# Operations put at the end of a step, and a 512-column matmul for both weight parts, in a hybrid decoder layer

## The chip, the cores and the metric

The kernel runs on one core of a Trainium2 chip. The metric is the device time of one execution in microseconds (us); the time of a version is the median of its runs. Engines are called TensorE (PE; its weight loads are PEld), VectorE (DVE), ScalarE (ACT), GpSimd (POOL) and the sync engine (SP), whose queue issues all transfers of this kernel.

## What is computed

One layer of a decoder over one prompt of 2048 tokens and eight sampled sequences of four tokens. Cut to what matters:

```python
mod = jnp.dot(jax.nn.silu(c), w_ada) + b_ada            # conditioning: shift, scale, gate
shift, scale, gate = jnp.split(mod, 3, axis=-1)
h = _rms(x, norm_g) * (1 + scale[:, None]) + shift[:, None]
proj = jnp.dot(h, w_in) + b_in                          # (T, 1024) x (1024, 7176)
hq, hf, hi, hz, mu, mz, mo, mi, mf = jnp.split(proj, SPLIT_IDX, axis=-1)
f = lb + (1.0 - lb) * jax.nn.sigmoid(hf)
o_h, S_new = _hgrn2(hq, jnp.log(f), hi, S_h, chunk)     # 8 heads, state 128 x 128
y_h = _head_rms(o_h, hgrn_norm_g) * jax.nn.silu(hz)
xc = jax.nn.silu(conv(mu) + conv_b)
q, k, v = _blockdiag(xc, wq), _blockdiag(xc, wk), _blockdiag(mu, wv)
h_m, C_new, n_new, m_new = _mlstm(q, k, v, mi, log_sigmoid(mf), C_m, n_m, m_m, chunk)  # 4 heads, 256 x 256
y_m = (_head_rms(sigmoid(mo) * h_m, mnorm_g) + skip * xc) * jax.nn.silu(mz)
out = x + gate[:, None] * jnp.dot(jnp.concatenate([y_h, y_m], -1), w_out)
```

## The kernel before

Every operand of the large products is held as two parts, a high part rounded to the matmul format and a low part that is the rest. A product is then three matmuls: high by high, low by high, high by low.

The prompt goes in four segments of 512 tokens, each in chunks of 128. A segment is a list of units. A narrow unit projects 128 columns of w_in (f, q, z, mu, mz) with the weights as the stationary operand and 512 tokens moving (`proj_ct`, line 543). A wide unit (v, mo) projects 256 columns with 128 tokens of h as the stationary operand and 256 columns of weights moving (`proj_tok`, line 556); its result is read by one addition of the bias (`evac`, line 1484), and the bias is loaded at the start of the unit into a tile with one buffer (`bias_bc`, line 1370). In one of the four head groups of a segment the 32 sampled tokens ride along. Weights are split in the first segment by ScalarE and GpSimd (`split`, line 205), kept in DRAM and read back in the later ones; four slots (tag w8) hold them, of which a wide unit takes two: one for the high part and one for the low part.

The order of the work is set by hand. `run_unit` steps the matmuls of a unit; after each step `pump` (line 576) first issues stores that are due and then lets every generator in `rec` go on to its next `yield`. The heads of both branches are such generators (`hgrn`, `hgrn_out`, `conv`, `mlstm`, `mlstm_out`), so the operations of several heads stand between the matmuls of a step, on every engine in the order in which the generators issue them, and each engine takes its instructions in order. All PSUM tiles come from one ring of eight banks (`ps_tile`).

```python
for g in list(rec):
    if next(g, "end") == "end":
        rec.remove(g)
```

Before the first unit the conditioning is computed (`ada_rows`, line 451): 16 pieces of w_ada, each split by ScalarE and by VectorE or GpSimd, two accumulators of 512 columns for each half, then the rows are transposed to columns (`ada_shift_scale`), x is scaled by GpSimd (`x_scale`), transposed, and modulated (`x_modulate`), and the weights of unit 0 are split (`stream_unit(0)`, line 1588). In the HGRN2 heads the state goes from chunk to chunk by an addition on VectorE and a scaling on GpSimd (`pscale`, lines 676 to 678). The block-diagonal weights are spread out by `bd_fill` on VectorE in the first segment (`bd_prep`). At the end of a segment x of the next one is loaded and scaled (`x_next`, line 1666) while the last unit runs. After the last segment the output projection follows (line 1743).

Of the kernel before, what the change touches and what calls it, by code (L numbers as in the profile page):

```python
# [8 lines left out]
F32 = mybir.dt.float32  # L9
# [8 lines left out]
P = 128  # L18
# [49 lines left out]
def hymba_step(ctx, tc, flag, halved, x_prompt, x_sample, c_prompt, c_sample, state_hgrn, state_C, state_n, state_m,  # L68
# [140 lines left out]
    class Unit:  # L209
# [11 lines left out]
        def alloc(self):  # L221
            if self.wide:
                self.hi = ring.tile([P, KD, 2 * P], F32R, tag="w8", name="whi", bufs=4)
                self.lo = ring.tile([P, KD, 2 * P], F32R, tag="w8", name="wlo", bufs=4)
                self.parts = [x.rearrange("p k m -> p (k m)") for x in (self.hi, self.lo)]
# [10 lines left out]
        def split(self, j):  # L236
# [4 lines left out]
            split(self.raw.pop(j), self.hi[:, :, c], self.lo[:, :, c], pool if self.src is w_in else vec)  # L241
# [7 lines left out]

    def C(nm, k):  # L250
        return cols[:, col[nm] + k:col[nm] + k + 1]
# [4 lines left out]
    sct = S2("sct", [P, KD, 1 + NSEQ])  # L256
# [4 lines left out]
    vec.tensor_tensor(sct[:, :, 1:], sgc[:, KD:].rearrange("p (s k) -> p k s", k=KD),  # L261
                      acol[:, 32:96].rearrange("p (s k) -> p k s", k=KD), op=ALU.mult)

    ML = 32 + 1 + NSEQ + 1
    scs = con.tile([P, KD, ML], F32R, name="scs")
    scp = S2("scp", [P, KD, ML])
    vec.memset(scp, 0.0)
    vec.tensor_copy(scs, scp)
    vec.tensor_copy(scs[:, :, :1 + NSEQ], sct)
    vec.tensor_tensor(scs[:, :, 32:33 + NSEQ], sct, scs[:, :, :1 + NSEQ].bitcast(F32), op=ALU.subtract)  # L270
# [172 lines left out]
    NB = 1 + NSEQ  # L443

    def ada_piece(n):
        k, b = divmod(n, 2)
        t = Bt("wada", [P, D]) if n % 2 else raw_tile()
        sync.dma_start(t, w_ada[k * P:k * P + P, b * D:b * D + D])
        return t

    def ada_rows(step):

        acc = [ps_tile("pada") if b % 2 else ps_tile("pada") for b in range(4)]
        raw = {n: ada_piece(n) for n in range(4)}
        for n in range(2 * KD):
            k, b = divmod(n, 2)
            step(n)
            r = raw.pop(n)
            t = ring.tile([P, 2, D], F32R, tag="w8", name="wadas", bufs=4)
            act(t[:, 0], r, AF.Copy)  # L460
            (pool if n % 4 == 3 else vec).tensor_tensor(t[:, 1], r, t[:, 0].bitcast(F32), op=ALU.subtract)
            for g in range(2):
                c = slice(512 * g, 512 * g + 512)
                for y in range(2):
                    pe.matmul(acc[2 * b + g][:ML], scs[:, k], t[:, y, c], start=(k == 0 and y == 0),
                              stop=(k == KD - 1 and y == 1))
            if n + 4 < 2 * KD:
                raw[n + 4] = ada_piece(n + 4)
        return acc

    def ada_shift_scale(acc):
        rows = Bt("arows", [NB, D])
        rows2 = Bt("arows", [NB, D])
        for b in range(4):
            dst = (rows, rows2)[b // 2][:, 512 * (b % 2):512 * (b % 2) + 512]
            act(dst, acc[b][:NB], AF.Copy)
            vec.tensor_tensor(dst, dst, acc[b][32:32 + NB], op=ALU.add)
        for r, dst, one in ((rows, msh, 0.0), (rows2, msc, 1.0)):
            ps = ps_tile("padt")
            for k in range(KD):  # L480
                pe.transpose(ps[:, k * NB:k * NB + NB], r[:, k * P:k * P + P], ident[:NB, :NB])
            v = ps[:, :KD * NB].rearrange("p (k b) -> p k b", k=KD)
            c0 = KD if one else 0
            vec.scalar_tensor_tensor(dst, v, one, acol[:, c0:c0 + KD, None].to_broadcast([P, KD, NB]),
                                     op0=ALU.add, op1=ALU.add)
        vec.tensor_tensor(msc, msc, C8("norm_g")[:, :, None].to_broadcast([P, KD, NB]), op=ALU.mult)

    def ada_gate(g, u):
# [6 lines left out]
        for k in range(KD):  # L495
            for w in (u.hi, u.lo):
                pe.matmul(ps[:ML, :Q], scs[:, k], w[:, k, :], start=(k == 0 and w is u.hi), stop=(k == KD - 1 and w is u.lo))
# [58 lines left out]
    def proj_tok(smp, u, evac):  # L556
        for c, t0, n in toks(smp):
            ps = ps_tile("ptok")
            i = 0
            for k in range(KD):  # L560
                if n == CH:
                    for w, h in ((u.hi, hhi), (u.lo, hhi), (u.hi, hlo)):
                        pe.matmul(ps[:, :2 * P], h[:, k, t0:t0 + n], w[:, k, :], start=(i == 0), stop=(i == 3 * KD - 1))  # L563
                        i += 1
                else:
                    for w in (u.hi, u.lo):
                        pe.matmul(ps[:2 * n, :2 * P], hhi[:, k, SEG:], w[:, k, :], start=(i == 0), stop=(i == 2 * KD - 1))
                        i += 1
# [5 lines left out]
    stores = deque()  # L574

    def pump(n=1):
        for _ in range(n):
# [6 lines left out]
            for g in list(rec):  # L584
                if next(g, "end") == "end":
                    rec.remove(g)

# [13 lines left out]
    def hgrn(s, h, d):  # L601
# [10 lines left out]
        vec.tensor_tensor_scan(G[:, :W], hmask[:, :W], G[:, :W], 0.0, op0=ALU.mult, op1=ALU.add)  # L612
        g4 = G[:, :SEG].rearrange("p (c u t) -> p c u t", u=2, t=CH // 2)
        mid = small("mid", [P, NCH, 1])
        vec.tensor_copy(mid, g4[:, :, 0, CH // 2 - 1:CH // 2])
        vec.tensor_tensor(g4[:, :, 0], g4[:, :, 0], mid.to_broadcast([P, NCH, CH // 2]), op=ALU.subtract)
        pool.tensor_scalar(tn[:, :W], tn[:, :W], noml[:, h:h + 1], oml[:, h:h + 1], op0=ALU.mult, op1=ALU.add)  # L617
# [11 lines left out]
        vec.tensor_tensor(beta[:, :NCH - 1], sm[:, 0:NCH - 1], sm[:, NCH + 1:2 * NCH], op=ALU.mult)  # L629
        vec.tensor_tensor(Ep[:, :W], hq[:, :W], Ep[:, :W], op=ALU.mult)  # L630
        vec.tensor_tensor(tn[:, :W], tn[:, :W], G[:, :W], op=ALU.mult)
# [37 lines left out]
        for c in range(NCH):  # L669
# [180 lines left out]
    def hgrn_out(s, h, po, ops):  # L850
# [4 lines left out]
        for c in range(NCH):  # L855
# [3 lines left out]
        vec.tensor_tensor(on[:, :SEG].rearrange("p (c v) -> p c v", c=NCH), po.rearrange("p (c v) -> p c v", c=NCH),  # L859
                          f[:, :, None].to_broadcast([P, NCH, CH]), op=ALU.mult)  # L860
# [12 lines left out]
        vec.tensor_tensor(sz[:, :W], sz[:, :W], y[:, :W], op=ALU.mult)  # L873
# [3 lines left out]
        vec.scalar_tensor_tensor(y[:, :SEG], pn, C("hg", h), sz[:, :SEG], op0=ALU.mult, op1=ALU.mult)  # L877
        if smp:
            pn = ps_tile("pn")
            pe.matmul(pn[:, :NSM], onesm, sq)  # L880
            act(sq, pn[:, :NSM], AF.Ln, bias=epsc)
            act(sq, sq, AF.Exp, scale=-0.5)
            vec.scalar_tensor_tensor(ops, ops, C("hg", h), sq, op0=ALU.mult, op1=ALU.mult)
            vec.tensor_tensor(y[:, SEG:], ops, sz[:, SEG:], op=ALU.mult)
        y_store(s, h, y, W)
# [122 lines left out]
    def conv(s, i, j, d):  # L1008
# [28 lines left out]
        vec.tensor_tensor(xc[:, :W], xc[:, :W], e[:, :W], op=ALU.mult)  # L1037
# [55 lines left out]
    def mlstm(s, i, d):  # L1093
# [10 lines left out]
        def head(c):  # L1104
# [6 lines left out]
            vec.tensor_tensor(dm[:, t], ps[:, :CH], dm[:, t], op=ALU.mult)  # L1111
            st = small("st", [P, 2, CH], 2, F32R)
# [759 lines left out]
```

## Time and profile before

| | |
|---|---|
| median of 3 runs | 2248.98 us (2247.84 to 2250.97) |
| the profiled execution's own time | 2243.03 us |
| its span, first to last instruction | 2241.2 us |
| mean granted TensorE clock | 0.989 of full speed |

The profile is of one execution. The span leaves out what lies before the first and after the last instruction. The matmuls overlap, and their ends are modelled: the time from the start of one to the start of the next is what one costs, not its duration.

### The profile page before, as it was taken

The page shows a single profiled execution, that of the slowest core. Times are in us where ns is not written, and L with a number is a line of the kernel's source. Part 1 is how long each engine was busy: PE and PEld are TensorE (multiplying, and loading weights), DVE is VectorE, ACT ScalarE, POOL GpSimd, SP SyncE. Part 2 cuts the span into 40 slices and gives each one's busy share as a digit, 9 for nine tenths or more (in the row PEclk, how much of TensorE's full clock was granted, in tenths as well). Part 3 has the DMA queues.
Part 4 walks back from the last instruction along what each step waited for, and adds up shares of the span by engine and source line. Part 5 has one row for each costly group of instructions (what it writes and reads, how often), then busy time and mean ns, then how long its engine had stood idle before and what let it go on. Part 6 is the DMA issues. An engine that isn't in the chain of part 4 may idle for free.

```text
span 2241.2 us, 35168 instructions
## 1 busy us (share of the span) xinstructions
PE 2170.0 (97%) x13594; PEld 1915.1 (85%) x13594; DVE 1268.8 (57%) x2664; ACT 979.1 (44%) x2260; POOL 432.0 (19%) x436
## 2 busy tenths in 40 slices
PE   6999999999999999999999999999999998999998
PEld 3888998787899889899988898888899987888885
DVE  7675657566756574566574555655455675423232
ACT  6445554464443354353444454534444535212121
POOL 3424353341112020212010212110101033000000
PEclk8999999999999999999999999999999999999999
DMA  7676766864546465634465555454555566533330
GB/s 257 214 234 219 262 221 205 302 227 155 189 152 228 167 230 193 217 136 158 179 203 202 189 192 180 162 169 163 146 194 161 174 193 173 165 108 96 93 99 27
DMA packets 225318, 405.26 MB, mean 181 GB/s; under 512 B 24843, under 2 KB 168627, under 8 KB 196470
## 3 DMA queue, kind: packets, MB, share of 16 engines
q1 hardware_dynamic: 225142, 402.92, 54.2%
q8 instruction: 109, 1.79, 0.3%
q14 instruction: 67, 0.55, 0.1%
HBM read 298.43 MB, written 104.44 MB: 180 GB/s over the span
## 4 chain that ended last, share of the span: by engine, by line
PE 68%; DVE 4%; ACT 3%; DMA 1%; issue 1%; POOL 1%; SPq 0%; DVEq 0%; ACTq 0%; POOLq 0%
PE pct L549 27%; PE pout L1743 15%; PE ptok L563 11%; PE p L1151 1%; PE pc L1135 1%; PE pv L1064 1%; PE pp L663 1%; PE pa L639 1%; PE pq L1081 1%; PE po L687 1%; PE po L689 1%; PE psx L1108 1%; ACT st L92 1%; PE p L1135 1%; DMA raw<-in_w_out_dram 1%
## 5 line engine op out<-in xcount | busy, mean ns | idle before, releaser
L549 PE MATMUL pct<-hhi,w 128*128 128x512 f32 (+1 forms) x3200 | 852.0, 354 | 1.2 <-DVE S L697 1.2
L549 PEld LDWEIGHTS pct<-hhi,w 128*128 128x128 f32 x3200 | 552.9, 188 | 74.4 <-issue 3.3
L549 PE MATMUL pct<-hlo,w 128*128 128x512 f32 (+1 forms) x1600 | 560.6, 350 | 0.0
L549 PEld LDWEIGHTS pct<-hlo,w 128*128 128x128 f32 x1600 | 301.0, 188 | 39.2
L563 PE MATMUL ptok<-whi,hhi 128*128 128x256 f32 x1024 | 301.4, 294 | 4.4 <-ACT hhi L92 3.3
L563 PE MATMUL ptok<-whi,hlo 128*128 128x256 f32 x1024 | 291.2, 284 | 0.2 <-DVE hlo L426 0.2
L563 PE MATMUL ptok<-wlo,hhi 128*128 128x256 f32 x1024 | 290.9, 284 | 0.0
L1743 PE MATMUL pout<-wh,y 128*128 128x512 f32 (+1 forms) x792 | 247.2, 391 | 3.0 <-ACT wh L92 3.0
L563 PEld LDWEIGHTS ptok<-whi,hhi 128*128 128x128 f32 x1024 | 197.4, 193 | 7.8 <-ACT hhi L92 3.7
L563 PEld LDWEIGHTS ptok<-wlo,hhi 128*128 128x128 f32 x1024 | 197.6, 193 | 2.3 <-issue 2.2
L563 PEld LDWEIGHTS ptok<-whi,hlo 128*128 128x128 f32 x1024 | 197.3, 193 | 0.9 <-DVE hlo L426 0.9
L1743 PEld LDWEIGHTS pout<-wh,y 128*128 128x128 f32 (+1 forms) x792 | 148.2, 187 | 35.8 <-ACT wh L92 3.5
L1743 PE MATMUL pout<-wl,y 128*128 128x512 f32 (+1 forms) x408 | 159.8, 392 | 1.1 <-POOL wl L1780 0.6
L92 ACT ACTIVATE xo<-oo 128x512 f32<-128x512 f32 (+1 forms) x34 | 21.5, 632 | 249.5 <-DVE oo L1831 249.5
L92 ACT ACTIVATE e<-e 128x512 f32<-128x512 f32 (+1 forms) x160 | 102.0, 638 | 58.9 <-DVE e L1034 54.8
L1826 DVE TENSOR_TENSOR oo<-pout,gate 128x512 f32<-128x512 f32 x32 | 22.0, 687 | 186.3 <-PE pout L1743 185.4
L617 POOL TENSOR_SCALAR tn<-tn,noml,oml 128x512 f32<-128x512 f32 (+1 forms) x32 | 52.6, 1643 | 385.5 <-ACT G L92 384.8
L207 POOL TENSOR_TENSOR w<-raw,w 128x1024 fp32r<-128x1024 f32 x40 | 97.2, 2436 | 113.5 <-ACT w L92 95.1
L121 POOL TENSOR_SCALAR num<-num,fin 128x256 f32<-128x256 f32 x64 | 35.1, 566 | 401.7 <-DVE fin L1313 357.8
L1161 DVE SCALAR_TENSOR_TENSOR Cc<-Cc,dec,pc 128x258 f32<-128x258 f32 x120 | 52.4, 478 | 84.0 <-PE pc L1135 84.0
L1743 PEld LDWEIGHTS pout<-wl,y 128*128 128x128 f32 (+1 forms) x408 | 75.6, 185 | 19.7 <-POOL wl L1780 1.3
L1032 DVE SCALAR_TENSOR_TENSOR xc<-mu,cols,xc 128x512 f32<-128x512 f32 (+1 forms) x120 | 83.7, 698 | 4.2
(403 smaller groups left out, 3792.2 us busy)
## 6 DMA issues: line engine op xcount, KB each, us to landing
w<-wdr SPq DMA_DIRECT2D x120, 1024.0 KB
wdr<-w SPq DMA_DIRECT2D x40, 1024.0 KB
raw<-in_w_in_dram SPq DMA_DIRECT2D x56, 512.0 KB
whi<-wdr SPq DMA_DIRECT2D x24, 1024.0 KB
wlo<-wdr SPq DMA_DIRECT2D x24, 1024.0 KB
raw<-ydr SPq DMA_DIRECT2D x29, 512.0 KB
xt<-in_x_prompt_dram SPq DMA_DIRECT2D x28, 512.0 KB
raw<-in_w_ada_dram SPq DMA_DIRECT2D x16, 512.0 KB
```

The costliest lines, as they stand in the source:

```text
L92: nc.scalar.activation(out, in_, func, bias=bias, scale=scale, **kw)
L121: pool.tensor_scalar(out, in_, sc, 0.0, op0=ALU.mult, op1=ALU.add)
L207: eng.tensor_tensor(lo, raw, hi.bitcast(F32), op=ALU.subtract)
L549: pe.matmul(ps[:, :n], w[:, k, :], h[:, k, t0:t0 + n], start=(i == 0), stop=(i == 3 * KD - 1))
L563: pe.matmul(ps[:, :2 * P], h[:, k, t0:t0 + n], w[:, k, :], start=(i == 0), stop=(i == 3 * KD - 1))
L617: pool.tensor_scalar(tn[:, :W], tn[:, :W], noml[:, h:h + 1], oml[:, h:h + 1], op0=ALU.mult, op1=ALU.add)
L639: pe.matmul(pa[:, t], kt[:, t], qt[:, t])
L663: pe.matmul(pp[:, c * CH:c * CH + CH], ktT[:, c], v[:, c, vc])
L1032: vec.scalar_tensor_tensor(o, src(r), C("cw", 8 * r + k), o, op0=ALU.mult, op1=ALU.add)
L1135: pe.matmul(out[:, :DH + 2], a[:, x], b[y][:, c], start=(q == 0), stop=(q == 2))
L1161: vec.scalar_tensor_tensor(Cc[:, j], Cc[:, j], dec[:, i, c:c + 1], pcs[j][:, :DH + 2], op0=ALU.mult, op1=ALU.add)
L1743: pe.matmul(acc[g][:n if n == CH else 2 * n], a, b[:, 512 * g:512 * g + 512], start=(k == 0 and q == 0), stop=(k == KO - 1 and q == len(mm ...
```

## The change

It has these parts.

1. A wide unit's two slots hold four of the eight k each, with high and low weights side by side. A token chunk takes per k one matmul of 512 columns (both parts, with the high part of h) and one of 256 (high weights, with the low part of h). The evacuation adds the second 256 columns with an operation of its own.
2. A queue `late`: closures appended in a step run after all generators of that step. In it go the scan and what follows it, the products after the exponentials, the normalised o, the z gate and its store, the product of xc, and in the mLSTM output the scaling and the gate.
3. The chain of R scales on VectorE; the fills of `bd_prep` go to GpSimd; the mLSTM `head` issues its ScalarE and VectorE operations in another order, and takes the split of C into itself.
4. The bias of a wide unit is loaded at the end of the wide unit before.
5. `ada_rows` multiplies eight unsplit fp32 pieces of 2048 columns, four matmuls each into four groups of 32 rows of one bank; the weights of unit 0 are split on VectorE.
6. x of the next segment is scaled one call later than it is loaded, behind the modulation.

```diff
-                self.hi = ring.tile([P, KD, 2 * P], F32R, tag="w8", name="whi", bufs=4)
-                self.lo = ring.tile([P, KD, 2 * P], F32R, tag="w8", name="wlo", bufs=4)
+                self.half = [ring.tile([P, KD // 2, 2, 2 * P], F32R, tag="w8", name="wh8", bufs=4) for _ in range(2)]
...
+        def both(self, k):
+            return self.half[k // 4][:, k % 4]
...
+            if self.wide:
+                for a, t in enumerate(self.half):
+                    split(raw[:, 4 * a:4 * a + 4], t[:, :, 0, c], t[:, :, 1, c], e)
...
-        acc = [ps_tile("pada") if b % 2 else ps_tile("pada") for b in range(4)]
-        raw = {n: ada_piece(n) for n in range(4)}
-        for n in range(2 * KD):
...
+        acc = ps_tile("pada")
+        w = {k: ada_load(k) for k in range(4)}
+        for k in range(KD):
+            step(k)
+            t = w.pop(k)
+            for q in range(4):
+                pe.matmul(acc[32 * q:32 * q + 32], sct[:, k], t[:, 512 * q:512 * q + 512], start=(k == 0),
+                          stop=(k == KD - 1), skip_group_check=True)
+            if k + 4 < KD:
+                w[k + 4] = ada_load(k + 4)
...
-                    for w, h in ((u.hi, hhi), (u.lo, hhi), (u.hi, hlo)):
-                        pe.matmul(ps[:, :2 * P], h[:, k, t0:t0 + n], w[:, k, :], start=(i == 0), stop=(i == 3 * KD - 1))
+                    mm = [(hhi, w.rearrange("p a m -> p (a m)")), (hlo, w[:, 0])]
+                    for i, (h, x) in enumerate(mm if k < KD - 1 else mm[::-1]):
+                        pe.matmul(ps[:, :x.shape[-1]], h[:, k, t0:t0 + n], x, start=(k == 0 and i == 0),
+                                  stop=(k == KD - 1 and i == 1), skip_group_check=True)
...
             for g in list(rec):
                 if next(g, "end") == "end":
                     rec.remove(g)
+            while late:
+                late.popleft()()
...
+        def decays():
+            vec.tensor_tensor_scan(G[:, :W], hmask[:, :W], G[:, :W], 0.0, op0=ALU.mult, op1=ALU.add)
+            vec.tensor_copy(mid, g4[:, :, 0, CH // 2 - 1:CH // 2])
+            vec.tensor_tensor(g4[:, :, 0], g4[:, :, 0], mid.to_broadcast([P, NCH, CH // 2]), op=ALU.subtract)
+            pool.tensor_scalar(tn[:, :W], tn[:, :W], noml[:, h:h + 1], oml[:, h:h + 1], op0=ALU.mult, op1=ALU.add)
+
+        late.append(decays)
...
+        def scaled():
+            vec.tensor_tensor(beta[:, :NCH - 1], sm[:, 0:NCH - 1], sm[:, NCH + 1:2 * NCH], op=ALU.mult)
+            vec.tensor_tensor(Ep[:, :W], hq[:, :W], Ep[:, :W], op=ALU.mult)
+            vec.tensor_tensor(tn[:, :W], tn[:, :W], G[:, :W], op=ALU.mult)
+
+        late.append(scaled)
...
-                pscale(nxt, u, sc)
+                vec.tensor_scalar(nxt, u, sc, None, op0=ALU.mult)
...
+        late.append(lambda: vec.tensor_tensor(
+            on[:, :SEG].rearrange("p (c v) -> p c v", c=NCH), po.rearrange("p (c v) -> p c v", c=NCH),
+            f[:, :, None].to_broadcast([P, NCH, CH]), op=ALU.mult))
...
+        def finish():
+            vec.tensor_tensor(sz[:, :W], sz[:, :W], y[:, :W], op=ALU.mult)
+            vec.scalar_tensor_tensor(y[:, :SEG], pn, C("hg", h), sz[:, :SEG], op0=ALU.mult, op1=ALU.mult)
...
+            y_store(s, h, y, W)
...
+        late.append(lambda: vec.tensor_tensor(xc[:, :W], xc[:, :W], e[:, :W], op=ALU.mult))
...
+            def scale(nm=nm, n=n, nch=nch, f=f):
+                vec.tensor_tensor(f[:n, 3, :nch], f[:n, 2, :nch], f[:n, 1, :nch], op=ALU.mult)
+                for c in range(nch):
+                    pscale(nm[:n, c, :DH], nm[:n, c, :DH], f[:n, 3, c:c + 1])
...
+    def bias_load(u):
+        while u < len(units) and units[u][1] not in ("v", "mo"):
+            u += 1
+        if u < len(units):
+            c0 = (OI if units[u][1] == "v" else OMO) + 2 * units[u][2] * P
+            bias[u] = small("bb", [P, 2 * P], 1)
+            sync.dma_start(bias[u], bcast_ap(b_in[0, c0:c0 + 2 * P], P))
...
                     vec.tensor_tensor(t[:, c], ps[:, :2 * P], bb, op=ALU.add)
+                    vec.tensor_tensor(t[:, c], t[:, c], ps[:, 2 * P:], op=ALU.add)
...
-                bd_fill(bo[:, (k - 2) % 4, 0], 2, k - 2, vec)
+                bd_fill(bo[:, (k - 2) % 4, 0], 2, k - 2, pool)
...
-    stream_unit(0)
+    stream_unit(0, vec)
...
             nxt[c] = x_load(s + 1, c)
+
+        def x_now(c):
             x_scale(s + 1, c, nxt[c][0], nxt[c][2])
```

## Rows read from the trace of the kernel before

**Rows 1.** The page: busy time of each engine, share of the span, instructions.

```profile
PE 2170.0 (97%) x13594; PEld 1915.1 (85%) x13594; DVE 1268.8 (57%) x2664; ACT 979.1 (44%) x2260; POOL 432.0 (19%) x436
```

**Rows 2.** Windows: stretch, its us, busy us of each engine, PEclk, DMA share, GB/s.

```profile
100.00:126.00 26.00, 20.80 (x101) 17.09 (x100) 23.89 (x50) 9.52 (x19) 10.39 (x7) 0.90 0.49 122
...
300.00:400.00 100.00, 94.05 (x756) 90.56 (x755) 66.01 (x132) 52.37 (x124) 43.70 (x27) 0.98 0.76 256
...
500.00:520.00 20.00, 15.99 (x116) 15.00 (x115) 11.52 (x25) 9.39 (x24) 5.21 (x6) 0.91 0.40 164
...
600.00:1500.00 900.00, 896.46 (x6065) 813.19 (x6064) 537.89 (x1196) 418.63 (x1022) 137.68 (x189) 1.00 0.54 187
...
1500.00:1560.00 60.00, 55.77 (x352) 50.13 (x351) 33.43 (x77) 26.80 (x57) 3.60 (x6) 0.94 0.44 148
```

**Rows 3.** Waits of TensorE over the whole span: us in total, times, longest us.

```profile
PE ph L1324 <- POOL num L121: 6.7, 4, 4.2
...
PE po L689 <- DVE R L674: 4.2, 3, 3.2
PE pb L1542 <- DVE bt L1554: 4.2, 1, 4.2
...
PE pxt L397 <- POOL xt L121: 1.8, 1, 1.8
...
PE ptok L563 <- DVE y L877: 1.1, 1, 1.1
```

**Rows 4.** Timeline of the start: start us, us, engine, line, operation, idle before.

```profile
35.51 1.21 DVE L461 TENSOR_TENSOR wadas<-raw,wadas 128x1024 fp32r<-128x1024 f32 x1
35.64 4.23 PE L465 MATMUL pada<-wadas,scs 128*42 128x512 f32 x11 [3.35 <-DVE wadas L461]
...
41.54 4.65 POOL L207 TENSOR_TENSOR wlo<-raw,whi 128x1024 fp32r<-128x1024 f32 x2 [7.03 <-ACT whi L92]
...
44.01 1.37 DVE L411 TENSOR_SCALAR hst<-pxt,msc,msh 128x128 f32<-128x128 f32 x4
...
45.45 1.16 ACT L92 ACTIVATE hhi<-hst 128x512 fp32r<-128x512 f32 x2
...
46.15 0.58 PE L563 MATMUL ptok<-whi,hhi 128*128 128x256 f32 x1 [3.27 <-ACT hhi L92]
```

**Rows 5.** Timeline of TensorE from 240 us, narrow unit and token chunk.

```profile
244.59 0.62 PE L549 MATMUL pct<-hhi,w 128*128 128x512 f32 x2
...
246.66 1.88 PE L1081 MATMUL pq<-xc,bm 128*128 128x512 f32 x4
...
251.15 0.28 PE L563 MATMUL ptok<-whi,hhi 128*128 128x256 f32 x1
...
254.02 0.60 PE L1108 MATMUL psx<-qp,xc 128*128 128x128 f32 x4
```

**Rows 6.** Windows, the instructions on pout alone.

```profile
1950.00:2000.00 50.00, 50.00 (x222) 41.41 (x221) 4.12 (x6) 0.00 (x0) 1.00 0.29 84
```

**Rows 7.** Groups by line and shape: busy us, mean ns, idle before, releasers.

```profile
L677 DVE TENSOR_TENSOR U<-R,pp 128x128 f32<-128x128 f32 x120 | 34.4, 287 | 60.7 <-POOL R L121 48.7 <-PE pp L663 11.5
...
L121 POOL TENSOR_SCALAR R<-U,beta 128x128 f32<-128x128 f32 x88 | 32.7, 372 | 245.4 <-DVE U L677 243.9 <-PE pz L990 0.5 <-PE pct L549 0.5
...
L612 DVE TENSOR_TENSOR_SCAN G<-hmask,G 128x512 f32<-128x512 bf16 x24 | 29.7, 1237 | 34.9 <-ACT G L92 34.8
...
L1486 DVE TENSOR_TENSOR v<-ptok,bb 128x256 f32<-128x256 f32 x64 | 26.8, 421 | 70.3 <-PE ptok L563 36.4 <-DMA bb<-in_b_in_dram 28.9 <-PE p L1151 3.5
```

**Rows 8.** Waits of the sync queue, first 60 us.

```profile
SPq L448 <- DVE wadas L461: 9.3, 4, 4.3
```

**Rows 9.** DMA view of the first 60 us: GB/s in 40 slices.

```profile
GB/s 0 21 104 396 421 418 413 411 407 401 399 407 396 367 417 385 279 68 339 378 289 90 332 412 221 147 203 11 0 2 210 163 13 21 116 386 431 393 291 310
```

**Rows 10.** Line 331, both engines: min/median/max ns, first and last start.

```profile
L331 DVE TENSOR_TENSOR bt<-bdw,oh x16: 277/282/1957, 73.1 to 154.6; 128x128 f32<-128x128 f32 x16
...
L331 POOL TENSOR_TENSOR bdf<-bdw,oh x8: 388/487/844, 1481.9 to 1840.2; 128x128 f32<-128x128 f32 x8
```

More of the change, by code (lines that the diff above doesn't have):

```diff
@@ L441, in toks, with ada_load @@
         return [(c, c * CH, CH) for c in range(NCH)] + ([(NCH, SEG, NSM)] if smp else [])
[L443 to L448, printed above, removed]
+    def ada_load(k):
+        t = ring.tile([P, 2 * D], F32, tag="w8", name="wada", bufs=4)
+        sync.dma_start(t, w_ada[k * P:k * P + P, :2 * D])
         return t
     def ada_rows(step):
-        acc = [ps_tile("pada") if b % 2 else ps_tile("pada") for b in range(4)]
-        raw = {n: ada_piece(n) for n in range(4)}
-        for n in range(2 * KD):
[L456 to L468, printed above, removed]
@@ L473, in ada_shift_scale @@
[L473 to L485, printed above, removed]
+        r = Bt("arows", [P, 512])
@@ L495, in ada_gate @@
         for k in range(KD):
-            for w in (u.hi, u.lo):
-                pe.matmul(ps[:ML, :Q], scs[:, k], w[:, k, :], start=(k == 0 and w is u.hi), stop=(k == KD - 1 and w is u.lo))
+            for y in range(2):
+                pe.matmul(ps[:ML, :Q], scs[:, k], u.both(k)[:, y], start=(k == 0 and y == 0), stop=(k == KD - 1 and y == 1))
         yield
@@ L574, in hymba_step @@
     stores = deque()
+    late = deque()
     def pump(n=1):
@@ L1137, in mlstm @@
         cur = head(0)
-        ch = None if first else c_split()
         yield
@@ L1368, in hymba_step @@
     start.append(len(units))
-    def bias_bc(c0):
-        t = small("bb", [P, 2 * P], 1)
-        sync.dma_start(t, bcast_ap(b_in[0, c0:c0 + 2 * P], P))
-        return t
+    bias = {}
+    def bias_load(u):
[5 more added lines that the diff above has]
+            sync.dma_start(bias[u], bcast_ap(b_in[0, c0:c0 + 2 * P], P))
     KO = 2 * D // P
@@ L1415, in stream @@
                 unit.alloc()
-            unit.split(j)
+            unit.split(j, eng)
             npiece[0] += 1
@@ L1481, in run_unit @@
             ts = small(kind + "s", [P, 2 * P], 1) if smp else None
-            bb = bias_bc((OI if kind == "v" else OMO) + 2 * n * P)
+            bb = bias.pop(u)
             def evac(ps, c, w):
@@ L1497, in run_unit @@
             pump(steps)
+        if kind in ("v", "mo"):
+            bias_load(u + 1)
         if kind == "q":
@@ L1569, in x_norm, with ada_step @@
         x_scale(0, c, x0[c][0], x0[c][2])
-    def ada_step(n):
-        if n < len(row_loads):
-            sync.dma_start(*row_loads[n])
-        if n in (1, 3):
-            x0.append(x_load(0, len(x0)))
-        if n in (6, 8):
-            x_norm(n // 2 - 3)
-        if n == 13:
+    pre = []
+    def ada_step(k):
+        if k < 4:
+            for d in row_loads[4 * k:4 * k + 4]:
+                sync.dma_start(*d)
+        if k == 0:
+            x0.append(x_load(0, 1))
+        if k in (2, 4):
+            x_norm(k // 2 - 1)
+        if k == 3:
+            gate_prep()
+        if k == 4:
+            pre.extend(x_transpose(x0[0][0], CH, g) for g in range(2))
+        if k == 5:
             cols_prep()
+    x0.append(x_load(0, 0))
     acc = ada_rows(ada_step)
-    assert len(row_loads) <= 13
+    assert len(row_loads) <= 16
     load_pieces(1)
@@ L1680, in hymba_step @@
                 x_next(1)
+            if j == per - 1 and not last:
+                x_now(0)
+                x_now(1)
             if j == (5 if s == 0 else 1 if last else 2):
```

133 lines of the change are left out of this document (67 added, 66 removed).

## Prediction

> **What bounds the kernel now.** I read the page's busy line first: TensorE is busy 97% of the span, VectorE 57%, ScalarE 44%, GpSimd 19% [rows 1]. So time can come only from TensorE: fewer or cheaper matmuls, less time in which it stands still, less time at its lower clock. VectorE, ScalarE and GpSimd matter only where TensorE waits for one of them.
>
> Then the stretch table, to see where TensorE stands still. From 600 to 1500 us it is busy 896.5 of 900 us at a granted clock of 1.00: reordering other engines cannot win more than 3.5 us there [rows 2]. It loses 5.2 us in 100 to 126, 6.0 in 300 to 400, 4.0 in 500 to 520 and 4.2 in 1500 to 1560, with means of the granted clock of 0.90, 0.98, 0.91 and 0.94 [rows 2]. A mean of 0.90 is a fifth of the stretch at 1.2 instead of 2.4 GHz, 5.2 us in which half the work is done, so some 2.6 us lost; the four together give 2.6 + 1.0 + 0.9 + 1.8 = 6.3 us.
>
> Then the list of what TensorE waits for: after the start the largest are the transposes ph behind a GpSimd scaling, 6.7 us, the bd transposes' products pb behind VectorE, 4.2, po behind a VectorE R, 4.2, and pxt behind GpSimd's scaling of x, 1.8 [rows 3]. No wait for a weight load or for a bias stands among them. The last view is the timeline of the start: the first token matmul begins at 46.15 us [rows 4].
>
> **The wide matmul.** For each of 128 token chunks (16 v and 16 mo units of 4) and each of 8 k, three 256-column matmuls become one of 512 columns and one of 256. Columns stay at 768; one weight load and one matmul go, 1024 of each. A chunk of 24 runs from 251.15 to 254.02 us, so 119.6 ns from start to start [rows 5]. For 512 columns of the same kind there are two rows: nine in 2.07 us (244.59 to 246.66), 230 ns [rows 5], and 222 in 50 us of the output stage, 225 ns [rows 6]. Three at 119.6 are 358.8 ns; the new pair is 225 to 230 + 119.6 = 344.8 to 349.6. That saves 9.2 to 14.0 ns, times 1024: 9.4 to 14.3 us. I take 12.
>
> By the rows a 256-column matmul costs 119.6 ns and one of twice the width under twice that, so some 10 to 14 ns belong to each matmul whatever its width. The Trainium skill, "TensorE: Matmul & The Clock Gate", section "Back-to-back issue gap", gives a warm matmul its columns at 2.4 GHz and some 2.5 ns more; by that the saving would be 2.6 us, an estimate from the page, and the forecast some 9 us higher. The page gives that gap for matmuls by themselves, and here every matmul has a weight load of its own; the rows are of these very operations, and they decide.
>
> The evacuation now takes two VectorE additions per chunk instead of one: 128 more of 0.42 us [rows 7], 54 us of VectorE. Its cover is VectorE's idle 43%; without it a PSUM bank would come free 0.42 us later per chunk, and eight banks rotate. I charge nothing. The other bound is 0.42 x 128 = 54 us, if every bank were needed at once; the list names one wait of a token matmul for VectorE's reading of a bank, 1.1 us [rows 3], so I stay at nothing. In the first segment the splits of v and mo weights come as two of half the width on ScalarE and GpSimd, which costs their idle time; the kept copies are as many transfers of the same size as before.
>
> **The start.** Now 16 pieces of w_ada are each split by ScalarE and by VectorE or GpSimd, and the sync queue waits 9.3 us for VectorE to free buffers [rows 8]. The last eleven matmuls run from 35.64 to 39.87, the first token matmul starts at 46.15 [rows 4]. The change loads eight pieces of 1 MB into four slots and multiplies them unsplit: no ScalarE or VectorE work between landing and matmul. Transfers run at about 400 GB/s once they flow, from the fourth bin of 1.5 us [rows 9]. Ahead of the last piece's end stand 8 x 1.05 MB and two x tiles of 0.52, 9.4 MB, some 23.5 us from about 4 us on: 28 us. The last four matmuls are fp32 of 512 columns; the nearest row is pq, four of which take 1.88 us [rows 5], twice that at half clock: to 31 us with the landing. Then one copy of 512 columns (about 0.7, from 0.42 for 256 [rows 7]), four transposes (0.6, as four matmuls of 128 take [rows 5]), three small additions (under 0.3 each by the U row [rows 7]) and their hand-overs: 33.5. VectorE then also makes the low parts of the first v unit, ahead of hst: four of half the size of one that takes 1.21 us, some 2.4, where GpSimd did it beside VectorE in 4.65 us; hst 1.37 and hhi 1.16 follow [rows 4]: with a hand-over 38.5 us. Saved: 46.15 - 38.5 = 7.5, rounded. Bounds: nothing, if the first weights land or are split too late, and 11, if the split lies beside the matmuls.
>
> **Operations put at the end of a step.** Per head the scan, mid copy, subtraction and the affine of tn (GpSimd), the three products, the on product, and the gate products with their store; per conv the xc product; in the mLSTM output the kap product with four GpSimd scalings, and the gate products with their store. They are issued after all generators of the step, so VectorE no longer stands at them while ScalarE works. It stands 34.9 us before the scan now [rows 7]. That is VectorE's time, not TensorE's. Each consumer stands two or more yields behind, so TensorE pays nothing where a step has slack. Their stores, one DMA per head and per half of an mLSTM head and a second where the samples ride along, go onto the sync queue up to a step later; only the output stage reads them.
>
> **R, fills, biases, x.** 120 scalings of the R chain (88 R and 32 Sc) go from GpSimd, 372 ns for an R [rows 7], to VectorE. An addition on tiles of this size takes 287 ns there [rows 7], so about 35 us more on VectorE, against 48.7 us that it stood waiting for GpSimd's R [rows 7]. po waits shrink: of 4.2 us [rows 3] with the dip of clock behind it I count 4. Of bd_prep, 24 fills go to GpSimd, 487 instead of 282 ns by the nearest rows [rows 10], off the VectorE that is busy 23.9 of 26 us when pb waits [rows 2, 3]: of 4.2 us and 2.6 of clock I count 2, as the gate work that fills VectorE there stays. Scaling x after the modulation, not ahead of it, takes GpSimd out of a wait for the load: of 1.8 us [rows 3] and its dip I count 2. The ph wait moves 1 us either way: kap comes late, but the products ahead of it do too. The 32 bias loads move to the end of the v or mo unit before. They wait there for the last evacuation, for bb has one buffer; behind them on the sync queue stand weight loads for units to come and stores, which no TensorE wait names. Where VectorE stood for bb, 28.9 us before v alone [rows 7], it no longer does. The head's new order in the mLSTM gives ScalarE work while VectorE makes dm; TensorE waits little there, 1 us. The sum is 4 + 2 + 2 + 1 = 9, less 2 for new waits: 7. Bounds: 20, some two thirds of the 5.2 + 6.0 + 4.0 + 4.2 us of standing and 6.3 of clock in the stretches above, and a loss, the last rival below.
>
> **Sum.** 12 + 7.5 + 7 = 26.5 us. The profiled execution took 2243.0 us (span 2241.2), so 2216.5 for such an execution. The runs shown have a median of 2249.0, 6 us above it; the same saving gives 2222.
>
> **Rivals.** *The wide matmul saves nothing:* cost goes by columns, 119.6 ns for 256 and so 239 for 512. The rows at 225 and 230 speak against it, though those have another operand moving. That leaves 14.5 us: 2234. The skill's 2.5 ns per matmul would give nearly this time.
>
> *The stalls fall with the start:* the waits before 600 us and at 1543 us vanish with their clock dips, 20 us instead of 7, and the start gives 10: 12 + 10 + 20 = 42, so 2207. For it speaks that VectorE's waits for ScalarE, GpSimd and biases all shrink; against it that the ph wait of 6.7 us hangs on a chain of ScalarE and GpSimd that is as long as before.
>
> *Late reads hold PSUM (slower):* po, pn and ph are read by operations that now come last in their step, behind all of VectorE's other work: 32 + 32 + 32 banks. If the next step's matmuls need such a bank, TensorE waits. From 26.5 / 96 = 0.28 us each the change is worth nothing; at 0.5 us each it costs 48, so 2249 - 26.5 + 48 = 2270. Against it: eight banks, some two allocated per step, and VectorE idle 43%. For it: VectorE gains 54 + 35 us of work. At 0.25 us each it gives no change: 2246.
>
> **How the numbers follow.** Forecast 0.52 (own range 2212 to 2232), stalls fall 0.16, wide matmul saves nothing 0.14, late reads eat the gain 0.06, late reads cost more 0.12. Within 0.2% (4.5 us, about what a measurement can tell) is only the fourth. So faster 0.82, same 0.06, slower 0.12. The range leaves out the last two and the far end of the second: 2202 to 2241.
>
> **What would show it.** Per chunk of the token matmuls 16 matmuls in 2.76 us instead of 24 in 2.87. The first of them near 38 us. No wait of TensorE for w_ada's low parts. From 600 to 1500 us busy time still above 99%. A wait of ptok, pct or psx for y, xs or on would mean the late reads; 512-column token matmuls 239 ns apart, the first rival; a first token matmul after 44 us, that the start was bound elsewhere.

## The result and the profile after

The changed kernel takes 2215.9 us (median of 4 runs, 2212.6 to 2217.9), the kernel before 2249.4 (4 runs, 2247.8 to 2251.0): a ratio of 0.985, 95% interval 0.9833 to 0.9867. The forecast was 2222 in a range of 2202 to 2241, so the sign came out as forecast, and the time 6 us below the forecast, inside the range. Between the profiled executions the saving is 2243.0 - 2217.9 = 25.1 us, against a forecast of 26.5; between the medians it is 33.5. The two differ because the profiled execution of before lies some 5 us below its runs, while that of after is the longest of its own.

The page's busy line after, where [rows 1] had before:

```profile
PE 2152.2 (97%) x12558; PEld 1850.7 (84%) x12558; DVE 1315.6 (59%) x2884; ACT 959.9 (43%) x2264; POOL 386.0 (17%) x349
```

TensorE has 1036 instructions fewer and is still busy 97% of the span: the bound has not moved. VectorE rose by 47 us, GpSimd fell by 46.

The windows of [rows 2] again, and one more (stretch, its us, then busy us of TensorE, its weight loads, VectorE, ScalarE and GpSimd, granted clock, DMA share, GB/s):

```profile
100.00:126.00 26.00, 21.42 (x110) 18.27 (x109) 23.50 (x51) 9.72 (x26) 12.83 (x14) 0.93 0.69 186
300.00:400.00 100.00, 95.29 (x695) 88.29 (x694) 74.11 (x162) 56.56 (x142) 38.57 (x23) 0.97 0.71 235
...
500.00:520.00 20.00, 18.07 (x111) 15.70 (x110) 14.38 (x38) 10.97 (x25) 1.24 (x4) 1.00 0.32 115
100.00:600.00 500.00, 482.68 (x2899) 418.12 (x2898) 342.27 (x731) 262.49 (x608) 177.05 (x134) 0.99 0.68 228
600.00:1500.00 900.00, 895.68 (x5579) 788.65 (x5578) 584.18 (x1346) 418.65 (x1031) 113.77 (x124) 1.00 0.54 185
1500.00:1560.00 60.00, 56.24 (x281) 46.67 (x281) 30.58 (x69) 22.51 (x48) 4.45 (x7) 0.94 0.50 175
```

Most stretches still have their holes, shrunk a little: 4.6 us of standing instead of 5.2 in the first, 4.7 instead of 6.0 in the second, 3.8 instead of 4.2 in the last. Only 500 to 520 is really mended, 1.9 instead of 4.0 with the clock at 1.00. The rows compare stretches of time and not of work: after, the work lies 8 us or more earlier. From 600 to 1500 TensorE stands 4.3 us instead of 3.5: more, not less, beside a VectorE that is busy 46 us longer there.

TensorE's waits over the whole span (us in total, times, longest us), to set beside [rows 3]:

```profile
PE pb L1574 <- DVE bt L1586: 4.5, 1, 4.5
PE ph L1343 <- POOL num L121: 4.4, 3, 3.8
PE ptok L563 <- ACT hhi L92: 3.9, 2, 3.4
PE po L700 <- DVE R L685: 3.9, 2, 2.6
...
PE pa L650 <- DVE tn L640: 3.1, 3, 1.9
...
PE pxt L409 <- POOL xt L121: 0.3, 1, 0.3
```

pb and po stand where they stood (4.2 each before); pxt fell from 1.8 to 0.3, ph from 6.7 to 4.4. The wait of a token matmul for VectorE's y is gone.

The timeline of the start after, beside [rows 4]:

```profile
29.16 1.93 PE L468 MATMUL pada<-wada,sct 128*32 128x512 f32 x8 [0.68 <-DMA wada<-in_w_ada_dram]
...
33.52 0.23 DVE L485 TENSOR_TENSOR msc<-msc,cols 128x72 f32<-128x72 f32 x1
33.70 2.50 DVE L207 TENSOR_TENSOR wh<-raw,wh 128x512 fp32r<-128x512 f32 x4
...
36.12 1.36 DVE L423 TENSOR_SCALAR hst<-pxt,msc,msh 128x128 f32<-128x128 f32 x4
...
37.51 1.15 ACT L92 ACTIVATE hhi<-hst 128x512 fp32r<-128x512 f32 x2 [2.15 <-DVE hst L423]
...
38.19 0.80 PE L563 MATMUL ptok<-wh,hhi 128*128 128x512 f32 x1 [3.40 <-ACT hhi L92]
```

The times that the forecast named can be read off: the w_ada matmuls end at 31.09 (forecast 31), shift and scale at 33.75 (33.5), the low parts take 2.50 (2.4), the first token matmul starts at 38.19 (38.5).

And a token chunk on TensorE after, as [rows 5] had one:

```profile
242.44 0.39 PE L563 MATMUL ptok<-wh,hhi 128*128 128x512 f32 x1
242.67 0.28 PE L563 MATMUL ptok<-wh,hlo 128*128 128x256 f32 x1
242.78 0.40 PE L563 MATMUL ptok<-wh,hhi 128*128 128x512 f32 x1
...
245.26 0.61 PE L1125 MATMUL psx<-qp,xc 128*128 128x128 f32 x4
```

Sixteen matmuls in 245.26 - 242.44 = 2.82 us, against 24 in 2.87 before and a forecast of 2.76.

### The profile page after: what moved, and what is told of

Read it like the earlier page. It is cut to its first block, busy times and chain, and to the rows that moved or that the text cites. A ratio compares the mean times of both kernels' runs of the same rounds, so it can differ in the third digit from the quotient of the medians.

```text
span 2216.1 us, 33304 instructions
## 1 busy us (share of the span) xinstructions
PE 2152.2 (97%) x12558; PEld 1850.7 (84%) x12558; DVE 1315.6 (59%) x2884; ACT 959.9 (43%) x2264; POOL 386.0 (17%) x349
## 4 chain that ended last, share of the span: by engine, by line
PE 78%; DVE 8%; DMA 5%; issue 3%; ACT 3%; POOL 2%; SPq 1%; POOLq 0%; DVEq 0%; ACTq 0%
PE pct L548 32%; PE pout L1790 15%; PE ptok L563 13%; PE p L1167 2%; PE pc L1152 2%; PE pv L1081 1%; PE po L700 1%; PE pq L1098 1%; PE po L698 1%; DMA wada<-in_w_ada_dram 1%; PE pa L650 1%; PE psx L1125 1%; PE pp L674 1%; DMA cs<-in_state_mlstm_C_dram 1%; PE p L1152 1%
## 5 line engine op out<-in xcount | busy, mean ns | idle before, releaser
L563 PE MATMUL ptok<-wh,hhi 128*128 128x512 f32 x1024 | 377.4, 408 | 3.9 <-ACT hhi L92 3.9
L563 PE MATMUL ptok<-wh,hlo 128*128 128x256 f32 x1024 | 267.5, 282 | 0.7 <-DVE hlo L438 0.7
L563 PEld LDWEIGHTS ptok<-wh,hhi 128*128 128x128 f32 x1024 | 191.1, 189 | 41.8 <-ACT hhi L92 4.6
L563 PEld LDWEIGHTS ptok<-wh,hlo 128*128 128x128 f32 x1024 | 194.5, 190 | 11.6 <-issue 2.2
L92 ACT ACTIVATE num<-p,zc 128x257 f32<-128x257 f32 x60 | 28.3, 472 | 148.0 <-PE p L1167 147.9
L1790 PE MATMUL pout<-wo,y 128*128 128x512 f32 (+1 forms) x328 | 76.8, 389 | 0.0
```

The source lines that it names most:

```text
L92: nc.scalar.activation(out, in_, func, bias=bias, scale=scale, **kw)
L563: pe.matmul(ps[:, :x.shape[-1]], h[:, k, t0:t0 + n], x, start=(k == 0 and i == 0), stop=(k == KD - 1 and i == 1), skip_group_check=True)
L1790: pe.matmul(acc[g][:n if n == CH else 2 * n], a, b[:, 512 * g:512 * g + 512], start=(k == 0 and q == 0), stop=(k == KO - 1 and q == len(mm ...
```

## Experiments

Every ratio below is to the kernel before, run beside it on the same chip; its medians there were 2245.5 to 2247.5 us. The changed kernel in that company takes 2214.6 (ratio 0.9854, 0.9833 to 0.9874), some 31 us less. Unless said otherwise an edit starts from the changed kernel and undoes one part of it, and no experiment leaves any part of the computation out. The mean granted clock of a version's runs lies between 0.986 and 0.992, at 0.989 for the changed kernel; 0.003 of 2216 us is up to 6 us, so a part of a small difference may be clock.

**The changed kernel again**, as the yardstick.

> The changed kernel itself, beside the others of this set, as their reference. Every theory: 2216 us, 33 less than the kernel before.

Measured 2214.6 us, ratio 0.9854 (0.9833 to 0.9874).

**Three 256-column matmuls again, with one addition.** The weights keep their new layout.

```
-  mm = [(hhi, both parts), (hlo, high part)]      # 512 and 256 columns
+  for i, (h, x) in enumerate(((hhi, w[:, 0]), (hhi, w[:, 1]), (hlo, w[:, 0]))):
+      pe.matmul(ps[:, :2 * P], h[:, k, t0:t0 + n], x, ...)
...
-  vec.tensor_tensor(t[:, c], t[:, c], ps[:, 2 * P:], op=ALU.add)
```

> The changed kernel, but each k of a token chunk takes three matmuls of 256 columns into the same columns again, with the new weight layout kept, and one evacuation addition. If the fixed cost of a matmul is what part 1 saves, this is 10 to 12 us slower than the changed kernel (2226 to 2228), as the start-to-start time goes from 350 ns per k to 359, 1024 times. If the saving is of columns and none is had (first rival), or 2.6 us as a fixed cost of 2.5 ns would give, it is 0 to 3 us slower. If the second addition on VectorE costs TensorE time, it may even be faster.

Measured 2217.8 us, ratio 0.9873 (0.9852 to 0.9894): 3 us behind the changed kernel, and the intervals overlap. So the pairing with its second addition, the part that the change is named for, is worth some 3 us and not shown apart from nothing, where the forecast had 12. Its timeline has the same chunk, right after the same narrow unit:

```profile
241.65 0.40 PE L562 MATMUL ptok<-wh,hhi 128*128 128x256 f32 x2
241.88 0.28 PE L562 MATMUL ptok<-wh,hlo 128*128 128x256 f32 x1
...
244.52 0.61 PE L1124 MATMUL psx<-qp,xc 128*128 128x128 f32 x4
```

2.87 us: the changed kernel's chunk is 0.05 us shorter, which is 6.4 us over 128 chunks. Over all 128 chunks of the two traces, each taken from its first token matmul to the next other matmul, it is 7.0 us. Something gives part of it back. One candidate is the clock, 0.992 in the mean of these runs against 0.989; the next run tries another.

**The same, with the bias addition done twice.** The second time it writes the same values once more, so the matmuls stay at three of 256 and VectorE has the 128 extra operations of the change.

```
   vec.tensor_tensor(t[:, c], ps[:, :2 * P], bb, op=ALU.add)
+  vec.tensor_tensor(t[:, c], ps[:, :2 * P], bb, op=ALU.add)
```

> Three matmuls of 256 columns per k, as in the run that undid the pairing (2217.8), but with the bias addition of each chunk done twice: 128 more VectorE operations of 0.42 us that change nothing. Theory: the second addition of the changed kernel is not free, it delays what stands behind it on VectorE (p waits for st), and takes back some 4 of the 7 us that the token matmuls save; then this is 3 to 5 us slower than that run, 2221 to 2223. Rival: VectorE's idle time covers it, as the prediction said, and this is within 1.5 us of 2217.8; then the pairing itself is worth only some 3 us.

Measured 2225.7 us, ratio 0.9909 (0.9895 to 0.9923): 8 us slower than without them, and 11 slower than the changed kernel, which has as many additions but pairs its matmuls. So the pairing by itself is worth some 11 us by the runs, and additions on an engine that is idle 40% of the time take 8 of them. The windows of the kernel with one addition:

```profile
600.00:1500.00 900.00, 898.75 (x6142) 818.97 (x6142) 556.80 (x1274) 419.13 (x1031) 113.42 (x124) 1.00 0.53 185
...
940.00:980.00 40.00, 40.00 (x318) 38.74 (x317) 26.54 (x66) 20.99 (x54) 2.62 (x4) 1.00 0.42 152
1380.00:1420.00 40.00, 40.00 (x257) 35.95 (x256) 29.00 (x69) 20.00 (x48) 3.28 (x8) 1.00 0.47 167
```

and with two:

```profile
600.00:1500.00 900.00, 894.39 (x6087) 812.95 (x6086) 580.99 (x1332) 413.08 (x1021) 114.33 (x124) 1.00 0.54 185
...
940.00:980.00 40.00, 38.50 (x304) 36.77 (x303) 30.35 (x72) 19.04 (x45) 3.83 (x4) 1.00 0.42 150
1380.00:1420.00 40.00, 38.13 (x259) 34.54 (x258) 29.72 (x73) 19.05 (x44) 2.34 (x6) 1.00 0.42 145
```

From 600 to 1500 us TensorE stands 5.6 us instead of 1.3. The two short stretches hold 3.4 of these 4.4 us: both lie at the end of a segment, where VectorE also modulates the next segment's x, and there the kernel with one addition has no hole at all. In the first of them TensorE's waits name the mLSTM's st, not the bank:

```profile
PE p L1151 <- DVE st L1141: 0.9, 2, 0.5
PE p L1151 <- ACT st L92: 0.5, 1, 0.5
```

So what the extra 0.42 us delays there is not the bank that it reads but the work behind it in VectorE's queue. Where the rest of the 8 us goes was not followed.

**The pairing alone, on the kernel before.** Weight layout, matmuls and second addition, nothing else.

> The kernel before with part 1 alone: the new weight layout, the 512-column matmul and the second addition. The prediction's term: 12 us faster than the kernel before. Theory now: token matmuls take 7 us less, and without the late queue the second addition gives back more than in the changed kernel: 0 to 4 us faster. Rival: it is slower than the kernel before.

Measured 2246.0 us beside 2245.8, ratio 0.9997 (0.9988 to 1.0007): nothing. Its windows:

```profile
100.00:600.00 500.00, 472.32 (x2805) 407.56 (x2804) 339.08 (x699) 255.80 (x585) 183.91 (x147) 0.98 0.64 215
600.00:1500.00 900.00, 893.54 (x5545) 785.41 (x5543) 565.22 (x1272) 418.97 (x1032) 140.06 (x192) 1.00 0.55 188
```

The kernel before is busy 476.7 us in the first stretch and 896.5 in the second: 4.4 + 2.9 = 7.3 us more of standing, which eats what the matmuls save.

**The addition spread over other engines.** ScalarE copies the low half, VectorE adds the high one, GpSimd adds the bias in SBUF.

```
-  vec.tensor_tensor(t[:, c], ps[:, :2 * P], bb, op=ALU.add)
-  vec.tensor_tensor(t[:, c], t[:, c], ps[:, 2 * P:], op=ALU.add)
+  act(t[:, c], ps[:, 2 * P:], AF.Copy)
+  vec.tensor_tensor(t[:, c], t[:, c], ps[:, :2 * P], op=ALU.add)
+  pool.tensor_tensor(t[:, c], t[:, c], bb, op=ALU.add)
```

> The changed kernel with another evacuation: ScalarE copies the low half of a chunk from PSUM, VectorE adds the high half, GpSimd adds the bias in SBUF. VectorE has one operation per chunk again, as before the change. Theory: the pairing saves 7 us of token matmuls, and the second VectorE addition cost 4 to 8 us of them; then this is 4 us or more faster than the changed kernel, 2208 to 2211. Rival: ScalarE's copy and GpSimd's addition delay others as much as VectorE's did, and this stays at 2214 to 2218.

Measured 2232.4 us, ratio 0.9936 (0.9923 to 0.995): 18 us slower. VectorE now stands in its own queue for the copy, and ScalarE's st comes late; the waits say so:

```profile
DVE v L1516 <- ACT v L92: 105.2, 45, 5.5
...
PE p L1152 <- ACT st L92: 5.6, 2, 3.1
```

These two waits of TensorE are 5.6 of the 18 us; the rest was not followed.

**Nothing late.** Every operation that the change puts at the end of a step is issued where it is written.

```
-  late = deque()
+  class AtOnce(list):
+      def append(self, f):
+          f()
+
+  late = AtOnce()
```

> The changed kernel, but every closure runs where it is appended instead of at the end of the step. My theory after the traces: TensorE is hardly held by VectorE in either order, so the time stays within 3 us of the changed kernel. Rival one, the late queue carries the gain at the first segment's end: 5 to 7 us slower, with the wait of a token matmul for y back at that boundary. Rival two, late reads hold PSUM: 5 us or more faster.

Measured 2227.8 us, ratio 0.9918 (0.9898 to 0.9937): 13 us slower than the changed kernel, more than any of the three expectations, and no wait of a token matmul for y is back. Its waits of TensorE, beside those of after shown above:

```profile
PE po L704 <- DVE R L689: 6.4, 3, 3.0
PE pa L654 <- DVE tn L644: 6.4, 5, 2.4
PE ph L1347 <- POOL num L121: 5.4, 4, 3.7
PE pb L1578 <- DVE bt L1590: 5.1, 1, 5.1
```

All four are longer (po 3.9, pa 3.1, ph 4.4, pb 4.5 after). And they lie early: the windows of this kernel

```profile
100.00:600.00 500.00, 474.87 (x2857) 413.33 (x2856) 343.80 (x731) 259.15 (x598) 176.56 (x132) 0.98 0.66 222
300.00:400.00 100.00, 93.30 (x698) 87.49 (x697) 70.92 (x150) 55.38 (x137) 41.31 (x23) 0.98 0.73 242
400.00:500.00 100.00, 93.67 (x494) 75.06 (x493) 70.16 (x151) 50.95 (x115) 35.94 (x25) 0.98 0.77 265
...
600.00:1500.00 900.00, 896.63 (x5575) 788.87 (x5574) 579.32 (x1335) 416.97 (x1028) 111.42 (x124) 1.00 0.54 186
```

have 7.8 us more of standing than after in 100 to 600, of which 2.0 in 300 to 400 and 3.0 in 400 to 500 (after: 96.67 busy), and none from 600 to 1500 (896.63 against 895.68). The longest wait of po can be followed in VectorE's queue, with nothing late:

```profile
460.11 0.89 DVE L1360 SCALAR_TENSOR_TENSOR xs<-ph,cols,xs 128x512 f32<-128x512 f32 x2
460.92 0.71 DVE L1362 TENSOR_TENSOR szm<-szm,e 128x544 f32<-128x544 f32 x1
461.66 0.73 DVE L1363 TENSOR_TENSOR xs<-xs,szm 128x544 f32<-128x544 f32 x1
462.31 0.35 DVE L689 TENSOR_SCALAR R<-pp,beta 128x128 f32<-128x128 f32 x1
...
462.71 0.52 PE L704 MATMUL po<-R,Ep 128*128 128x128 f32 x2 [3.02 <-DVE R L689]
```

and at the same place in the changed kernel:

```profile
455.69 0.33 DVE L685 TENSOR_SCALAR R<-pp,beta 128x128 f32<-128x128 f32 x1
...
457.87 0.90 DVE L1356 SCALAR_TENSOR_TENSOR xs<-ph,cols,xs 128x512 f32<-128x512 f32 x2
```

VectorE does not stand there. Without the queue 2.2 us of work on xs and szm, from 460.11 to 462.31, go ahead of the R that TensorE needs; with it R goes first, and no wait of po is listed there.

**Nothing late, with VectorE light**: three matmuls and one addition, and R scaled on GpSimd.

> The changed kernel without both additions to VectorE's work (three matmuls of 256 and one addition per chunk; R scaled on GpSimd) and without the late queue. Theory: the late queue is worth 13 us in the changed kernel because VectorE has more to do there; without that work its worth falls to some 5 us, and this takes 2220 to 2224. Rival: the queue's worth does not depend on it, and this is 13 us above the run with three matmuls (2217.8): 2231. Second rival: it is worth nothing here, 2216 to 2218.

Measured 2225.6 us, ratio 0.9916 (0.9901 to 0.9931). Against the kernel with three matmuls and late operations (0.9873; its R is scaled on VectorE, which is worth nothing by a run below) that is 0.0043, some 10 us; by the medians 8. So the late queue does not owe its worth to VectorE's added work alone: most of it is there with the light VectorE too.

**The old start**: sixteen split pieces of w_ada, four accumulators, the first weights split with GpSimd, and the old order of x loads and transposes between them.

```
-  w = {k: ada_load(k) for k in range(4)}          # 1 MB pieces, multiplied unsplit
+  raw = {n: ada_piece(n) for n in range(4)}       # half of it, split in two parts
...                                                # and what hangs on it
-  stream_unit(0, vec)
+  stream_unit(0)
```

> The changed kernel with the start of the kernel before: 16 split pieces of w_ada, low parts of the first weights on GpSimd. My theory, from the first token matmul at 38.2 us instead of 46.2 and the first narrow matmul 7.5 us earlier: 7 to 8 us slower than the changed kernel, 2222. Rival: the earlier start runs into half clock and transfers, and gives part back by the end of the first segment: 3 us slower or less.

Measured 2222.9 us, ratio 0.9899 (0.9884 to 0.9914): 8 us slower by medians, 10 by ratios. Its first token matmul starts at 45.60 us, 7.4 after that of the changed kernel.

**x scaled when it is loaded**, as before.

```
   def x_next(c):
       nxt[c] = x_load(s + 1, c)
-
-  def x_now(c):
       x_scale(s + 1, c, nxt[c][0], nxt[c][2])
...                                # the calls of x_now go
```

> The changed kernel, but x of the next segment is scaled right at its load again, ahead of the modulation. My theory: GpSimd waits some 16 us for a transfer at the first segment's end as before, holds hhi, and the changed kernel loses 5 us there (2221), 6 with the other two boundaries. Rival: the boundary gain is the late queue's or the bias load's, and this is within 2 us of the changed kernel.

Measured 2218.1 us, ratio 0.9863 (0.9841 to 0.9885): 2 us slower by ratios, 3.5 by medians, inside the intervals, so not shown apart from nothing. Its trace shows a place for it all the same. Two waits of token matmuls for VectorE stand in its list and not in that of the changed kernel, both just before 500 us:

```profile
PE ptok L563 <- DVE y L896: 1.9, 1, 1.9
...
PE ptok L563 <- DVE mo L1516: 1.0, 1, 1.0
```

So it is the later scaling, and not the late queue, that did away with the wait for y of the kernel before.

**R and Sc scaled on GpSimd**, as before.

```
-  vec.tensor_scalar(nxt, u, sc, None, op0=ALU.mult)
+  pscale(nxt, u, sc)
```

> The changed kernel with the 120 scalings of the R chain on GpSimd again. The prediction counted 4 us for them. My theory now: the wait of po for R is as long in both profiles (4.2 and 3.9 us), so the move gives nothing, within 2 us of 2215. Rival: it gives what the prediction said, 2219. Second rival: 35 us of VectorE are worth more than 49 us of its waits, and this is 2 to 4 us faster.

Measured 2213.0 us, ratio 0.9855 (0.984 to 0.987): the same as the changed kernel. The change did what it says to VectorE; after, its group of U (busy us, mean ns, idle before, releasers), beside U in [rows 7], is

```profile
L688 DVE TENSOR_TENSOR U<-R,pp 128x128 f32<-128x128 f32 x120 | 34.5, 287 | 18.3 <-PE pp L674 12.7 <-POOL dm L1102 1.8 <-POOL R L121 0.4
```

VectorE stands 18.3 us before U instead of 60.7, and none of it reaches the end.

**The bias loaded where its unit starts**, as before.

```
   bb = bias.pop(u)                # now loaded just ahead of this line
-  if kind in ("v", "mo"):
-      bias_load(u + 1)            # at the end of the unit
```

> The changed kernel with the bias of a wide unit loaded at the start of that unit again. Theory: VectorE stands 46 us for these loads in the kernel before, and as VectorE delays TensorE at the ends of segments, this costs 3 to 5 us: 2218 to 2220. Rival: the wait falls into VectorE's idle time, as the prediction had it: within 1.5 us of 2215.

Measured 2214.1 us, ratio 0.9857 (0.9841 to 0.9872): the same.

**A try at better**: R on GpSimd, and the copies that pb waits for on ScalarE.

```
-  vec.tensor_scalar(nxt, u, sc, None, op0=ALU.mult)
+  pscale(nxt, u, sc)
...
-  vec.tensor_copy(t[:, 2:4], ps[:, :2 * P]...)
+  act(t[:, 2:4], ps[:, :2 * P]..., AF.Copy)
```

> A version meant to beat both: the changed kernel with R scaled on GpSimd, and the eight copies bt of bd_prep on ScalarE, which is busy 4 of the 16 us around the wait of pb, where VectorE is busy 15.5. Theory: pb no longer waits 4.4 us behind VectorE, and some of the half clock behind it goes: 5 us faster than the run with R on GpSimd (2213), 2208. Rival: ScalarE waits there itself 8.9 us for VectorE's G, so the copy comes as late: 2213.

Measured 2214.2 us, ratio 0.9858 (0.9841 to 0.9874): the same. The wait of pb is gone from the list, and another has grown (3.9 us after, 3.1 with R alone on GpSimd):

```profile
PE po L700 <- DVE R L685: 7.1, 2, 4.0
```

No kernel tried here beats the changed one by more than can be measured.

## Why the prediction was right, and where it was not

Sign, size and bound were right; the terms that make up the sum were not all what I took them for. The table sets them beside what undoing each of them cost. Undone parts don't add up exactly: 26 of 31 us by medians, 32 of 33 by ratios.

| term | forecast us | measured us |
|---|---|---|
| wide matmul | 12 | 6 by the chunk shown, 7 by all chunks, 11 by the runs |
| its second addition | nothing | -8 |
| start | 7.5 | 8 to 10 |
| operations put at the end of a step | nothing | 13, with a light VectorE 8 to 10 |
| R on VectorE | 4 | nothing |
| x scaled later | 2 | 2 to 3.5, not shown apart from nothing |
| bias loads | nothing | nothing |
| fills, the mLSTM head's order, new waits | 2, 1 and -2 | not tried by themselves |

*The start* held in its sum, and in its steps from the copy on. Ahead of that two misses cancel, which is luck. The forecast has the last piece landed at 28 us and its four matmuls done by 31, though by its own row they take 3.8 us at half clock, to 31.8. The trace has TensorE wait for a piece until 29.16, and from there two pieces take 1.93 us together.

*The wide matmul* failed at "I charge nothing" for the second addition. Cover was read from VectorE's idle 43% over the whole span, and the wait list named hardly any token matmul waiting for a bank; both are right, and neither is the question. An added operation delays everything behind it in its engine's queue, and at the two segment ends shown that queue had no slack: 128 of 0.42 us, 54 us of work, cost 8 us, a seventh of the far bound. The 12 for the matmuls themselves stands up better, but was too much: 11 by the runs with two additions each, 7.0 by all chunks and 6.4 by the chunk shown, where the pairs come 352 ns apart instead of 344.8 to 349.6. What the runs have beyond the chunks stays open. The rival that goes by columns gives 359 and nothing saved; its tell, 512-column matmuls 239 ns apart, I chose badly. From a 512-column matmul to the next start it is indeed 230 to 250 ns there, 239 in the mean, but from a 256-column one it is 114, not 119.6. Only the sum of a pair tells.

By the rule that I cited, the Trainium skill, "TensorE: Matmul & The Clock Gate", section "Back-to-back issue gap", each matmul saved would give 2.5 ns, an estimate from a gap that the page gives for matmuls by themselves. For these, each with a weight load of its own, the trace doesn't agree: the chunk gives 6.3 ns for each (2.87 - 2.82 us over 8), all chunks 6.8, the runs 11 (11 us over 1024). The forecast's 9 to 14 was nearer, and too high by the traces.

*The late operations* failed at "TensorE pays nothing where a step has slack", and at leaving it there: I did not ask which steps have none. In 300 to 400 us VectorE is busy 74 us in 100, from 600 on 65, and in the former what stands ahead of R, tn and bt in VectorE's queue holds up TensorE, which waits for them in turn. Issued last, it holds up nothing of its own step. In the one wait that was followed, what stood ahead was work that TensorE did not wait for, and not a wait of VectorE for ScalarE. The prediction's "VectorE no longer stands at them while ScalarE works" holds for the product `on` above all, where VectorE's standing for ScalarE fell from 28.5 us to 2.9, most of it after 600 us, where TensorE had little to gain. At the scan it stands as long as ever, 46.4 us for ScalarE's G after the change and 45.4 before. My reading rests on the longer waits, on where they lie and on that one; that the order of the other operations does it, and not the later stores that move along, was not tried apart. The rival that late reads hold PSUM is out for the changed kernel: no wait of TensorE for y, xs or on stands in the list after, and the sign is the opposite. With x scaled early such a wait is there, the 1.9 us for y.

*R* was counted at 4 and is worth nothing: po still waits 3.9. The row of that wait names VectorE's R, not GpSimd's [rows 3]: the first of a chain, which VectorE scaled before the change too; I took VectorE's standing for GpSimd, idle time of an engine that isn't the bound, for its cause. *pb* kept its 4.2 us as well, so the fills bought nothing by this wait, and the try at better shows that even without it the time is unchanged, with po's wait longer instead.

*The clock* in the prediction's first paragraphs has a slip: the first stretch is charged its whole loss, 2.6 us, the other three half of theirs. By the same rule they are 2.0, 1.8 and 3.6, and the sum is 10.0 instead of 6.3. It enters the bound of 20 alone, which is two thirds of the larger sum and not of the one written.

The large misses, nothing counted where 8 were lost and nothing where 8 to 13 were won, nearly cancel; that the sum came out 6 us from the time is in good part luck. What stays open is the rest, some 1 to 5 us: the fills and the mLSTM head's new order were not tried by themselves, nor how much the late queue covers of the second addition's cost. That it covers some is suggested by the pairing's worth: nothing on the kernel before, some 3 us with the rest of the change.

## What to carry to other kernels

Cover for an added operation is read from the stretches where its queue is full, not from the engine's share of the span, and its price is what stands behind it in that queue. Where an in-order engine has work in its queue that the bound engine does not wait for, issuing it behind what that engine does wait for can be worth more than removing instructions from the engine that is the bound, and it costs no work. When a wait is removed, ask first what the engine would wait for next: pb's wait was taken away, po's grew, and the time stayed.

## What the runs showed of the hardware

Four fp32 matmuls of 512 columns, each with 32 columns of weights and its own quarter of the output's partitions, take the time of one. The timeline of w_ada's matmuls after, three pieces of four, and the window around them, where the granted clock is 0.50:

```profile
25.69 2.78 PE L468 MATMUL pada<-wada,sct 128*32 128x512 f32 x12
...
26.00:29.00 3.00, 2.48 (x12) 0.27 (x8) 0.00 (x0) 0.00 (x0) 0.00 (x0) 0.50 1.05 355
```

Three pieces take 2.78 us and two take 1.93, as shown for the start, so one more piece of four costs 0.85 us. For single fp32 matmuls of 512 columns over all partitions there is pq before, where four take 1.88 us [rows 5] and the last three of them

```profile
247.09 1.45 PE L1081 MATMUL pq<-xc,bm 128*128 128x512 f32 x3
```

so one costs 0.43 us at full clock, and 0.86 at half, an estimate from this row. I had charged four times that for a piece. The other surprise is told above: how long a matmul with its own weight load holds the next one back depends on the width of both, 239 ns and 114 in mixed pairs, 119.6 among 256-column ones.
